# First layer's result turned to channel rows: half of it by VectorE blocks and SBUF-to-SBUF transfers in place of TensorE

## The chip, the core and the metric

The kernel runs on one core of a Trainium2 chip. The metric is the device time of one execution in microseconds (us). Before the change it is 2030.38 us, the median of three runs (2029.91 to 2031.34). The engines are named as the profile names them: PE (TensorE, matmuls; PEld is its weight load), DVE (VectorE), ACT (ScalarE), POOL (GpSimd), SP (the queue that issues almost all transfers).

## What is computed

A decoder of two layers over 256 tokens of 2048 channels, all in float32. The first layer ends with a gated feed-forward network that is added to the residual stream `x`; the second layer begins with three projections of that stream, each behind an RMS norm whose scale is applied later, to the product:

```python
for l in range(DEPTH):
    if l == N_A:                                    # l == 1
        kv = rmsnorm(x, g_kv) @ w_kv_a              # first product of the second layer
        ...
    h = rmsnorm(x, g_mix[l])
    ...
    x = x + conv_ffn(rmsnorm(x, g_ffn[l]), w_ffn_up[l], conv_w[l], conv_b[l], w_ffn_down[l])
return rmsnorm(x, g_final)
```

## The kernel before

**Two layouts.** The products of the second layer want the stream by channels: 128 channels on the partitions, 16 such blocks of 256 tokens. The tile `k.x` (named `xT` in the trace) holds it so. The down-projection of the feed-forward network is computed the other way round: 128 tokens on the partitions, two such halves `tb`, 2048 channels along the row. Its running sum is the tile `xt` (class `Tokens`, line 1345). So between the first layer's feed-forward network and the second layer the stream has to be turned from tokens to channels.

**Split operands.** Every float32 product is made of three passes over rounded pieces. ACT rounds an operand (`hi`), DVE subtracts the rounded part from it (`lo`). Weights are treated so per 128x1024 block: transfer into `raw`, then ACT writes `whi`, then DVE writes `wlo`. `raw` and `whi` have 4 buffers each, so SP can load a block only when DVE is done with the one four blocks earlier. The stream's pieces for the products are in `xhl`, two tiles of eight channel blocks each, `[hi | lo]` per block.

**The end of the first layer's network.** The down-projection runs in two phases, `ph` 0 (channels 0 to 1023) and `ph` 1 (channels 1024 to 2047), for each of three groups of hidden units. In the last group phase 1 goes through six weight chunks, n = 0 to 5, of 24 matmuls of 512 columns each (lines 795 to 797). At its start DVE still adds what phase 0 gave to `xt` (`combine`, recorded under line 1391 with its lambda, and `added`, line 1407). Channels 0 to 1023 are complete with that. Phase 1's own four accumulators, `e00`, `e01`, `e10` and `e11`, are added to `xt` by line 1407 after chunk 5; the figure after `e` is the token half, the last one the column half.

**Turning.** `Inner.turned(k0)` turns two channel blocks: four PE transposes of 128x128 into one PSUM bank (line 406, in `token_transpose`), then ACT rounds the bank into `xhl` (1441), DVE writes the rest (1442), and ACT copies the bank into `k.x` (1443). Four calls, for channel blocks 0 to 7, are hooks behind chunks n = 1 to 4 of phase 1. The other four, for blocks 8 to 15, are hooks behind the first two chunks of the second layer's first product (`k.pending`, 1457). The square sums of the norm come from `xt` itself (1430).

**The first product of the second layer.** `gemm_fm` with `w_kv_a` (line 1140): eight weight chunks of two channel blocks each, 24 matmuls of 256 columns per chunk (lines 157, 158 with `hi` weights, 160 with `lo` weights). Chunk c needs `xhl` of blocks 2c and 2c+1. Its weights go through line 108 (SP), 123 (ACT) and 124 (DVE).

**What sets the order.** A scheduler orders each engine's instructions around here; each engine then works through its own list strictly in order. `keep_in_program_order` pins an instruction among its engine's others.

**A turn by blocks** in the other direction exists already: `Tokens.turn` (1361) turns channels to tokens before the network, with DVE transposes of 32x32 blocks and 4 transfers each from SP that put the blocks in place (1368).

Of the kernel before, what the change touches and what calls it, by code (L numbers as in the profile page):

```python
# [8 lines left out]
F32 = mybir.dt.float32  # L9
# [3 lines left out]
AF = mybir.ActivationFunctionType  # L13
ALU = mybir.AluOpType
AX = mybir.AxisListType

P = 128
D = 2048
S = 256
NB = D // P  # L20
# [1319 lines left out]
class Tokens:  # L1340
# [37 lines left out]
    def begin(self, ph, last):  # L1378
        self.ph, self.last = ph, last
        if ph == 0:  # L1380
            self.staged = self.k.ap.tile([P, 2, 4, 512], F32, tag="xT", name=self.k.uid("staged"))
        return {}
# [38 lines left out]
class Inner(Tokens):  # L1421
    def begin(self, ph, last):
        super().begin(ph, last)
        return {"hooks": {n: [lambda n=n: self.turned(2 * n - 2)] for n in range(1, 5)}} if last and ph else {}

    def evict(self, tb, half, acc):
        j, o = self.added(tb, half, acc)
# [3 lines left out]

    def turned(self, k0):
        k, nc = self.k, self.nc
        if k0 == 0:
            k.new_hl()
            k.x = k.ap.tile([P, NB, S], F32, tag="xT", name=k.uid("xT"))

        def put(b, acc):
            a = acc.rearrange("p (k s) -> p k s", k=2)
            hl = k.hl_tiles[b // 8][:, b % 8 : b % 8 + 2, :]  # L1440
            nc.scalar.activation(hl[:, :, :S], a, AF.Copy)
            nc.vector.tensor_tensor(hl[:, :, S:], a, hl[:, :, :S].bitcast(F32), ALU.subtract)
            nc.scalar.activation(k.x[:, b : b + 2, :], a, AF.Copy)

        k.token_transpose(self.xt, k0, k0 + 2, put)
# [111 lines left out]
```

## Time and profile before

| | |
|---|---|
| median of three runs | 2030.38 us |
| span of the profiled execution, first to last instruction | 2027.8 us |
| what lies around the span, against the median | 2.6 us |
| granted TensorE clock, mean of the span | 0.999 |
| PE / PEld busy | 99% / 94% |
| DVE / ACT / POOL busy | 80% / 58% / 6% |
| DMA: moved, mean rate | 409.24 MB, 202 GB/s |

All queries below have times counted from the start of the span. In a timeline row come the start, the time from the first start to the last end, engine, line, operation, output<-input and how many instructions are merged. Matmuls overlap: one of 512 columns is listed with 0.39 us, but they start 0.23 us apart. In the chain of work that ended last a row has the time by which the chain moved on. The profiled execution's own time outside of the span is not recorded, so sums are made on the span and set against the median with the 2.6 us.

### The profile page before, as it was taken

How to read it: one execution, taken by the hardware profiler on the slowest of the kernel's cores; microseconds unless marked ns; L12 is line 12 of the kernel's file. 1: busy time of each engine (PE TensorE's matmuls, PEld its weight loads, DVE VectorE, ACT ScalarE, POOL GpSimd, SP SyncE). 2: the span in 40 equal slices, each digit the busy share in tenths (PEclk: the TensorE clock that was granted, in tenths of full speed). 3: DMA queues.
4: the chain of work that ended last, by engine and by line, in shares of the span. 5: the costliest groups of instructions: out<-in, count | busy, mean ns of one | idle time of the engine just before them, and what ended most of it. 6: DMA issues, size and time to landing. Idle time of an engine off the chain costs nothing.

```text
span 2027.8 us, 38053 instructions
## 1 busy us (share of the span) xinstructions
PE 2017.2 (99%) x15136; PEld 1912.3 (94%) x15136; DVE 1618.2 (80%) x2433; ACT 1167.1 (58%) x1675; POOL 112.8 (6%) x169
## 2 busy tenths in 40 slices
PE   9999999999999999999999999999999999999998
PEld 8989999999889999899989999999988999889996
DVE  6866766778898788987878786777889878898787
ACT  6754744545565555655566675455566555565565
POOL 0000013100000000000002141400000000000000
PEclk9999999999999999999999999999999999999999
DMA  8876556688657676577656634568865767657764
GB/s 255 234 216 181 166 193 195 192 209 259 208 177 218 198 240 199 179 216 246 187 179 187 183 113 162 190 196 210 257 205 181 219 192 246 196 177 219 241 206 145
DMA packets 248263, 409.24 MB, mean 202 GB/s; under 512 B 71502, under 2 KB 78996, under 8 KB 248084
## 3 DMA queue, kind: packets, MB, share of 16 engines
q1 hardware_dynamic: 247892, 406.27, 65.4%
q8 instruction: 118, 1.93, 0.4%
q14 instruction: 61, 0.50, 0.1%
q10 hardware_dynamic: 192, 0.54, 0.1%
HBM read 400.46 MB, written 2.10 MB: 199 GB/s over the span
## 4 chain that ended last, share of the span: by engine, by line
PE 99%; DVE 0%; ACT 0%; issue 0%; ACTq 0%
PE ps L157 22%; PE ps L158 22%; PE ps L160 22%; PE ps L796 7%; PE ps L797 7%; PE ps L795 7%; PE ps L189 2%; PE ps L190 2%; PE ps L191 2%; PE ps L524 1%; PE ps L406 0%; PE ps L604 0%; PE ps L602 0%; PE ps L603 0%; PE ps L1236 0%; PE ps L1024 0%
## 5 line engine op out<-in xcount | busy, mean ns | idle before, releaser
L118 ACT ACTIVATE whi<-raw 128x1024 fp32r<-128x1024 f32 x484 | 512.7, 1061 | 513.1 <-PE ps L158 373.6
L119 DVE TENSOR_TENSOR wlo<-raw,whi 128x1024 fp32r<-128x1024 f32 x484 | 599.0, 1241 | 246.6 <-ACT whi L118 244.1
L157 PE MATMUL ps<-xhl,whi 128*128 128x256 f32 x3264 | 763.1, 277 | 0.0
L158 PE MATMUL ps<-xhl,whi 128*128 128x256 f32 x3264 | 761.5, 276 | 0.0
L158 PEld LDWEIGHTS ps<-xhl,whi 128*128 128x128 f32 x3264 | 612.8, 188 | 0.5
L157 PEld LDWEIGHTS ps<-xhl,whi 128*128 128x128 f32 x3264 | 612.7, 188 | 0.6
L160 PE MATMUL ps<-xhl,wlo 128*128 128x256 f32 x3264 | 436.6, 276 | 0.0
L160 PEld LDWEIGHTS ps<-xhl,wlo 128*128 128x128 f32 x3264 | 400.5, 188 | 0.0
L710 DVE TENSOR_TENSOR wlo<-raw,whi 128x1024 fp32r<-128x1024 f32 x112 | 134.3, 1220 | 31.5 <-ACT whi L709 30.3
L796 PE MATMUL ps<-wlo,h 128*128 128x512 f32 x404 | 157.3, 390 | 0.0
L797 PE MATMUL ps<-whi,h 128*128 128x512 f32 x404 | 157.2, 389 | 0.0
L709 ACT ACTIVATE whi<-raw 128x1024 fp32r<-128x1024 f32 x112 | 115.7, 1055 | 53.1 <-PE ps L158 37.3
L795 PE MATMUL ps<-whi,h 128*128 128x512 f32 x404 | 128.8, 390 | 0.0
L157 PE MATMUL ps<-mainhl,whi 128*128 128x256 f32 x512 | 119.7, 277 | 0.0
L158 PE MATMUL ps<-mainhl,whi 128*128 128x256 f32 x512 | 119.3, 276 | 0.0
L890 ACT ACTIVATE c<-a,cT 128x256 f32<-128x256 f32 x176 | 99.7, 592 | 32.2 <-DVE a L237 30.2
L709 ACT ACTIVATE whi<-xs 128x1024 fp32r<-128x1024 f32 x52 | 53.8, 1059 | 87.3 <-DVE xs L757 73.1
L158 PEld LDWEIGHTS ps<-mainhl,whi 128*128 128x128 f32 x512 | 96.0, 188 | 0.0
L157 PEld LDWEIGHTS ps<-mainhl,whi 128*128 128x128 f32 x512 | 95.9, 188 | 0.0
L795 PEld LDWEIGHTS ps<-whi,h 128*128 128x128 f32 x404 | 75.8, 188 | 15.7
L797 PEld LDWEIGHTS ps<-whi,h 128*128 128x128 f32 x404 | 75.8, 188 | 15.7
L796 PEld LDWEIGHTS ps<-wlo,h 128*128 128x128 f32 x404 | 75.9, 188 | 15.4
(378 smaller groups left out, 2896.6 us busy)
## 6 DMA issues: line engine op xcount, KB each, us to landing
raw<-in_w_ffn_up SPq DMA_DIRECT2D x352, 512.0 KB, 4.4
raw<-in_w_ffn_down SPq DMA_DIRECT2D x126, 512.0 KB, 4.5
raw<-in_w_out SPq DMA_DIRECT2D x64, 512.0 KB, 3.9
raw<-in_w_in_a SPq DMA_DIRECT2D x56, 512.0 KB, 4.2
gate<-in_w_ffn_down SPq DMA_DIRECT2D x38, 512.0 KB, 4.6
raw<-in_w_mem_kv SPq DMA_DIRECT2D x31, 512.0 KB, 4.8
sums<-in_w_ffn_down SPq DMA_DIRECT2D x48, 256.0 KB, 7.1
raw<-in_w_in_b SPq DMA_DIRECT2D x16, 512.0 KB, 4.1
```

Of the source, the lines that this page charges most:

```text
L118: nc.scalar.activation(hi[:, :n], raw[:, :n], AF.Copy)
L119: nc.vector.tensor_tensor(lo[:, :n], raw[:, :n], hi[:, :n].bitcast(F32), ALU.subtract)
L157: mm(acc[:, :S], wh, x[:, :S], start=first, stop=False)
L158: mm(acc[:, :S], wh, x[:, S:], start=False, stop=False)
L160: mm(acc[:, :S], wl, x[:, :S], start=False, stop=last)
L189: mm(acc, xh, wh, start=first, stop=False)
L709: self.behind(self.nc.scalar.activation(hi, w, AF.Copy))
L710: self.behind(self.nc.vector.tensor_tensor(lo, w, hi.bitcast(F32), ALU.subtract))
L795: mm(o, xh, wh, start=start, stop=False)
L796: mm(o, xh, wl, start=False, stop=False)
L797: mm(o, xl, wh, start=False, stop=stop)
L890: nc.scalar.activation(c, a, AF.Identity, scale=w(2), bias=w(3))
```

## The change

The four calls for channel blocks 0 to 7 go. In their place:

- `blocks(h)`, h = 0 and 1, as hooks behind chunks n = 0 and 1 of phase 1. Each is two DVE transposes (one per token half) of 128x512 in 32x32 blocks from `xt` into a scratch tile `xs`, and 16 transfers of 32 partitions x 8 runs of 32 elements (32 KB, 256 runs of 128 B) from `xs` into `k.x`. h = 0 covers channel blocks 0 to 3 and goes out on POOL's queue; h = 1 covers blocks 4 to 7 and goes out on SP's.
- `operand(b)` for b = 0, 2 as a hook behind chunk 4 and b = 4, 6 behind chunk 5: ACT rounds two blocks of `k.x` into `xhl`, DVE writes the rest. The copy into `k.x` by ACT (1443 before) is no longer needed for these blocks.

Blocks 8 to 15 are turned by PE as before.

```diff
 class Inner(Tokens):
     def begin(self, ph, last):
         super().begin(ph, last)
-        return {"hooks": {n: [lambda n=n: self.turned(2 * n - 2)] for n in range(1, 5)}} if last and ph else {}
+        if not (last and ph):
+            return {}
+        hooks = {h: [lambda h=h: self.blocks(h)] for h in range(2)}
+        hooks.update({n: [lambda b=b: self.operand(b) for b in range(4 * (n - 4), 4 * (n - 3), 2)] for n in (4, 5)})
+        return {"hooks": hooks}
+
+    def blocks(self, h):
+        k, nc = self.k, self.nc
+        if h == 0:
+            k.new_hl()
+            k.x = k.ap.tile([P, NB, S], F32, tag="xT", name=k.uid("xT"))
+        xs = k.tmp(self.pool, [P, 1024], "xs", 2)
+        s = xs.rearrange("p (r k a j) -> p r k a j", r=4, k=4, a=2)
+        for a in range(2):
+            src = self.xt[:, a, 512 * h : 512 * (h + 1)].rearrange("p (k r j) -> p r k j", r=4, j=32)
+            k.tc.keep_in_program_order(nc.vector.transpose(out=s[:, :, :, a], in_=src))
+        for r in range(4):
+            o = k.x[32 * r : 32 * (r + 1), 4 * h : 4 * (h + 1)].rearrange("i k (a q j) -> i q (k a) j", a=2, j=32)
+            for q in range(4):
+                (nc.sync if h else nc.gpsimd).dma_start(out=o[:, q], in_=s[32 * q : 32 * (q + 1), r].rearrange("i k a j -> i (k a) j"))
+
+    def operand(self, b):
+        k, nc = self.k, self.nc
+        x, hl = k.x[:, b : b + 2, :], k.hl_tiles[b // 8][:, b % 8 : b % 8 + 2, :]
+        nc.scalar.activation(hl[:, :, :S], x, AF.Copy)
+        nc.vector.tensor_tensor(hl[:, :, S:], x, hl[:, :, :S].bitcast(F32), ALU.subtract)
```

In `turned` the three lines that made `xhl` and `k.x` at `k0 == 0` go too. Lines behind the insertion move by 22 to 25: the squares (1430 before) are 1455 in the changed kernel, the adds stay 1407.

The scheduler moves work with it, all of it between chunk 0 of phase 1 and the first half of the product with `w_kv_a`; the order elsewhere is the same. PE at the seam of the two layers, before (`ps_12070` is the accumulator `e11`, `ps_12365` and on those of the product, `xhl_12143` the pieces of blocks 0 to 7):

```order
L797 MATMUL ps_12070<-whi_12295,hhx_1502_10099 128x512
L157 MATMUL ps_12365<-xhl_12143,whi_12370 128x256
L158 MATMUL ps_12365<-xhl_12143,whi_12370 128x256
L157 MATMUL ps_12365<-xhl_12143,whi_12370 128x256
L158 MATMUL ps_12365<-xhl_12143,whi_12370 128x256
```

and PE there in the changed kernel (`xhl_12107` the pieces of blocks 0 to 7, `ps_12447` to `ps_12503` the banks of the four turns of blocks 8 to 15):

```order
L797 MATMUL ps_12070<-whi_12305,hhx_1502_10099 128x512
L157 MATMUL ps_12379<-xhl_12107,whi_12384 128x256
L157 MATMUL ps_12380<-xhl_12107,whi_12384 128x256
L157 MATMUL ps_12381<-xhl_12107,whi_12384 128x256
L157 MATMUL ps_12382<-xhl_12107,whi_12384 128x256
L406 MATMUL ps_12447<-ident,xt 128x128 x4
L406 MATMUL ps_12455<-ident,xt 128x128 x4
L406 MATMUL ps_12495<-ident,xt 128x128 x4
L406 MATMUL ps_12503<-ident,xt 128x128 x4
L158 MATMUL ps_12379<-xhl_12107,whi_12384 128x256
```

Four products with `hi` of block 0 now stand ahead of the turns of blocks 8 to 15, which have moved up from behind the second and third chunk of the product; the rest of the first chunk stands behind them.

ACT around the seam in the changed kernel (1448 is the rounding of two blocks from `k.x`, first the pair 0 to 3, then 4 to 7; 123 the weights of the product; 1455 the squares):

```order
L123 ACTIVATE whi_12416<-raw_12415,gT 128x512 x2
L1455 ACTIVATE src_12338,fsums<-xt 128x512
L1448 ACTIVATE xhl_12107<-xT_12110 128x2x256 x2
L1455 ACTIVATE src_12341,fsums<-xt 128x512
L123 ACTIVATE whi_12464<-raw_12463,gT 128x512 x2
L123 ACTIVATE whi_12512<-raw_12511,gT 128x512
L1455 ACTIVATE src_12344,fsums<-xt 128x512
L123 ACTIVATE whi_12512<-raw_12511,gT 128x512
L1455 ACTIVATE src_12347,fsums<-xt 128x512
L1448 ACTIVATE xhl_12107<-xT_12110 128x2x256 x2
```

Before, the four roundings of blocks 0 to 7 (1441) stood one by one among the weights of chunks 3 to 5 of phase 1. Now they stand in two pairs, after the first square and after the last, and DVE's list has the matching subtractions (1449) at the same places, the first pair between the adds of `e10` and `e11`.

SP's list there in the changed kernel (`raw_12383` to `raw_12543` are the first five loads of `w_kv_a`):

```order
L108 DMA raw_12383<-in_w_kv_a 128x2x512
L108 DMA raw_12415<-in_w_kv_a 128x2x512
L108 DMA raw_12463<-in_w_kv_a 128x2x512
L1443 DMA xT_12110<-xs_12166 32x8x32 x16
L108 DMA raw_12511<-in_w_kv_a 128x2x512
L108 DMA raw_12543<-in_w_kv_a 128x2x512
```

Before, the five loads followed one another; now 16 transfers stand between the third and the fourth. On POOL's list the other 16 stand ahead of the fill and the adds with which it prepares the second layer (1098, 1107); nothing else of POOL stands near.

More of the change, by code (lines that the diff above doesn't have):

```diff
@@ L1433, in turned @@
         k, nc = self.k, self.nc
-        if k0 == 0:
-            k.new_hl()
-            k.x = k.ap.tile([P, NB, S], F32, tag="xT", name=k.uid("xT"))
         def put(b, acc):
```

## The prediction

> **What bounds the kernel now.** I read the page first: busy shares, clock and the chain that ended last.
>
> ```profile
> PE 2017.2 (99%) x15136; PEld 1912.3 (94%) x15136; DVE 1618.2 (80%) x2433; ACT 1167.1 (58%) x1675; POOL 112.8 (6%) x169
> PEclk9999999999999999999999999999999999999999
> PE 99%; DVE 0%; ACT 0%; issue 0%; ACTq 0%
> ```
>
> PE is busy for 2017.2 of 2027.8 us at full clock, and the chain runs through PE alone. So an instruction taken off PE is worth its own time on PE, and anything that makes PE wait costs its full length: there is no slack elsewhere to absorb it. Then I read the stretch of the change, first in a table by windows.
>
> ```profile
> 1042.00:1047.00 5.00, 5.00 (x26) 4.11 (x25) 3.63 (x4) 4.89 (x10) 0.00 (x0) 1.00 0.63 204
> 1047.00:1058.00 11.00, 11.00 (x54) 9.11 (x53) 6.29 (x9) 6.73 (x10) 0.00 (x0) 1.00 0.31 96
> 1058.00:1062.00 4.00, 4.00 (x23) 3.42 (x22) 3.36 (x6) 2.99 (x7) 0.00 (x0) 1.00 0.75 216
> ```
>
> The columns are window, length, then PE, PEld, DVE, ACT and POOL busy, clock, DMA share, GB/s. PE has no gap here either. DVE and ACT have some room, POOL does nothing, and the DMA engines are less than a third busy from 1047 to 1058.
>
> **What is removed.** The 16 PE transposes of channel blocks 0 to 7, in the chain of work:
>
> ```profile
> 1037.72 0.11 PE ps L406
> 1041.51 0.33 PE ps L406 x3
> 1043.70 0.44 PE ps L406 x4
> 1049.61 0.44 PE ps L406 x4
> 1055.54 0.43 PE ps L406 x4
> ```
>
> That is 0.11 + 0.33 + 0.44 + 0.44 + 0.43 = **1.75 us** off the chain. The other 16 transposes move up but stay, 8 of them at 0.87:
>
> ```profile
> 1066.90 0.87 PE ps L406 x8
> 1061.28 0.28 PE L157 MATMUL ps<-xhl,whi 128*128 128x256 f32 x1
> 1061.40 0.28 PE L158 MATMUL ps<-xhl,whi 128*128 128x256 f32 x1
> ```
>
> The second of these rows is the first matmul of the product with `w_kv_a`. It can now stand at 1061.28 - 1.75 = **1059.53**. This is the time by which `xhl` of block 0 has to be rounded, and so the time by which POOL's 16 transfers have to be in.
>
> **When POOL can start.** DVE's rows before that:
>
> ```profile
> 1036.59 1.22 DVE L710 TENSOR_TENSOR wlo<-gate,whi 128x1024 fp32r<-128x1024 f32 x1
> 1037.72 0.68 DVE L1407 TENSOR_TENSOR xt<-ps,xt 128x512 f32<-128x512 f32 x1
> 1040.59 1.28 DVE L1407 TENSOR_TENSOR xt<-ps,xt 128x512 f32<-128x512 f32 x2
> L1364 DVE STREAM_TRANSPOSE xs<-xT x8: 1235/1240/1245, 412.5 to 1388.6; 128x1024 f32<-128x1024 f32 x8
> ```
>
> The same transposition takes 1.24 us for 1024 columns, so 0.62 for 512. The first one stands ahead of the row at 1036.59, the second behind the work that ends at 1040.59: 1040.59 + 2 x 0.62 = **1041.8**. Every transfer of the half needs both. The other two transposes follow the weights of chunk 3. Four of them add 2.5 us to DVE, in windows where it was idle for 1.4 and 4.7 us, and each `wlo` then still stands some 2 us ahead of its matmul; I cost them at nothing. The four subtractions have the same size as before, and ACT loses four copies of 0.6 us.
>
> **When POOL's half must be in.** Behind a landing at L stand ACT's two roundings, DVE's two subtractions and, behind these on DVE, the add of `e11`, for which the last two turns on PE wait.
>
> ```profile
> L1441 ACT ACTIVATE xhl<-ps x8: 574/590/600, 1043.5 to 1071.8; 128x512 fp32r<-128x512 f32 x8
> 1067.38 1.09 ACT L1441 ACTIVATE xhl<-ps 128x512 fp32r<-128x512 f32 x2
> 1068.12 1.28 DVE L1442 TENSOR_TENSOR xhl<-ps,xhl 128x512 fp32r<-128x512 f32 x2
> ```
>
> The roundings end at L + 0.6 and L + 1.1, the second subtraction at L + 1.8, the add (0.68) at L + 2.45. PE wants its result behind four matmuls (4 x 0.11) and eight transposes (0.87): 1059.53 + 0.45 + 0.87 = 1060.85. So a landing by **1058.4** costs nothing, and a later one costs what it is late. From 1041.8 that leaves 16.6 us.
>
> **What 16 transfers on POOL's queue take.** No row of before shows a transfer issued by POOL. The nearest rows are SP's:
>
> ```profile
> L1368 SPq DMA_DIRECT2D xt<-xs x32: 591/667/3811, 413.9 to 1398.8; - x32
> 413.87 4.12 SPq L1368 DMA_DIRECT2D xt<-xs  x4
> L399 SPq DMA_DIRECT2D xraw<-in_x x32: 560/625/1169, 26.7 to 61.6; - x32
> DMA to landing us min/median/max: 3.7/3.9/5.3
> 1040.70 7.12 SPq L108 DMA_DIRECT2D raw<-in_w_kv_a  x4
> L1107 POOL TENSOR_TENSOR both<-ident x8: 252/253/257, 1072.0 to 1073.5; 128x32 f32<-128x32 f32 x8
> L279 POOL TENSOR_TENSOR sq<-xT x30: 612/789/1598, 288.7 to 1316.3; 128x256 f32<-128x256 f32 x30
> ```
>
> An issue of SP in the same form (32 partitions, short runs) takes 0.63 to 0.67 us; four in a row take 4.12, which is 1.03 each, since one waited. POOL's own instructions take 0.25 to 1.6 us. So I bound one POOL issue by 0.25 from below and 1.6 from above, and take the mean of the back-to-back row, **1.03**. The landing row belongs to line 399: 3.9 us from issue, reading HBM while the DMA engines were busier. For the last landing here I take 3.0 (an estimate, from that row and the low DMA share of the windows). Then L = 1041.8 + 15 x 1.03 + 3.0 = 1060.25, **1.85 us** late.
>
> The Trainium skill, "DMA: Bandwidth & Descriptors", section "Latency and other measured facts", gives about 0.6 us to the first byte for transfers from SP and ACT and about 1 us for those from GpSimd, whose descriptors software makes. By an estimate with 1 us per issue the half would land 0.45 us earlier, 1.4 late; no run here shows a POOL transfer yet.
>
> **What 16 transfers on SP's queue take.** They wait for DVE's last two transposes, at about 1046.5 by the same addition, and stand ahead of the fourth load of `w_kv_a`. In the row above SP issued the first four loads between 1040.70 and 1047.82; now the fourth comes 16 x 0.42 to 16 x 0.67 = 6.7 to 10.7 us after 1046.5, at the latest at 1057.2. It lands 3.6 to 4 us later, near 1061. PE needs that chunk at 1059.53 + 1.75 + 3 x 2.72 = 1069.4 (24 matmuls at 0.113). ACT has more behind it: two weight halves, two squares, then the roundings of blocks 4 to 7, together 4 us, and PE wants these at 1066.7. Near 1061 leaves about 1.5 us, so I cost SP's half at nothing. At 1.03 per issue the load would land at 1066.6 and PE would wait about 4 us, less what POOL's half has already cost.
>
> **Sum.** 2027.8 - 1.75 + 1.85 = 2027.9 on the span; with the 2.6 us between span and median, **2030.5 us**.
>
> **Rivals.**
>
> *The full gain.* If a POOL issue takes at most (16.6 - 3.0) / 15 = 0.91 us, nothing waits: 2030.4 - 1.75 = **2028.6**. For it speaks that SP's undisturbed issues take 0.67, and that these transfers have a quarter of the runs. Against it, that POOL is not SP, and that its own small jobs reach 1.6.
>
> *POOL's half is far too late.* From (16.6 + 5.75 - 3.0) / 15 = 1.29 us per issue on, PE waits longer than 5.75 us and the kernel is slower by over 4 us. At 1.6 the half lands at 1068.8, 10.4 late: **2039**. The place to see it is PE's first row of line 157 at the seam. For it speaks that nothing covers the wait, since PE's list has nothing but these four matmuls ahead of the turns.
>
> *DVE keeps POOL from its work.* If POOL could make transfers only while DVE is idle, it would have, from 1042 to 1059.5, the 1.37 + 4.71 + about 0.3 us that the windows leave. At 1.03 per issue 16.5 us are needed; the other 10 would come once DVE itself waits for ACT and ACT for POOL, so the half would land near 1072.5, 14 late: **2043**. Against it speaks that POOL's adds ran elsewhere at 0.6 to 1.6 us with DVE 80% busy.
>
> The Trainium skill, "SBUF — State Buffer", section "SBUF: two separate sides", has this as the trap "DVE blocks DMA": some VectorE modes lock GpSimd out while it writes descriptors. The same page says that `tensor_tensor` has no such mode, and DVE's work here is nearly all of that kind, so I give it little.
>
> *SP's weights come late*, as worked out above: at 1.03 per issue about 2 us on top of the forecast, **2032.5**.
>
> **How the numbers follow.** Forecast, POOL late by up to 5.75 us: 0.38. Full gain: 0.33. POOL far too late: 0.20. DVE in the way: 0.05. SP late: 0.04. About 0.2%, 4 us, is what a measurement of this kernel can tell from no change. The whole gain is 1.75 us, so faster than that bound can't come out of any case but a mismeasured one: 0.03. Slower are the two late cases and the tail of the forecast with SP's delay on top, 0.27; within the bound the rest, 0.70. The range has the full gain and the spread of the runs (0.5) at its low end, 2028.0, and the 1.6 us issue at its high end, rounded up to 2040; beyond lies the case of DVE.
>
> **What would show it.** Line 406 with `xt` has 16 matmuls left, and the chain loses 1.75 us between 1037 and 1059. A row of POOL's transfers, from about 1042 on, shows the cadence: up to 0.91 us the first rival is right, near 1.03 the forecast, over 1.29 the second. The wait of PE for ACT's line 1448 at the seam should be some 2 us; with none, the time should be 2028.6. The fourth load of `w_kv_a` should be issued by 1057 and no PE wait should stand behind the first chunk of that product. I am wrong in kind if PE waits for a weight (SP's queue) or for a `wlo` that a DVE transpose has pushed back.

## The result, and the profile after

The changed kernel takes 2036.9 us (median of 6 runs, 2036.07 to 2037.59), the kernel before 2029.95 in the 6 runs beside it: ratio 1.0032, 95% interval 1.0021 to 1.0043. It is **7 us slower**. The profiled execution has a span of 2034.3 us, before 2027.8. The forecast was 2030.5 with a range of 2028.0 to 2040.0: the time is in the range, but beyond the 4 us bound, and not by the mechanism that was given the most weight.

From the page of the changed kernel, the busy row of PE and the chain's shares by engine, then the row of PE's groups where idle time stands behind the last bar:

```profile
PE 2016.6 (99%) x15120; PEld 1911.6 (94%) x15120; DVE 1620.8 (80%) x2437; ACT 1164.8 (57%) x1671; POOL 122.1 (6%) x185
PE 96%; DVE 1%; DMA 1%; ACT 1%; issue 1%; SPq 0%; ACTq 0%; DVEq 0%
L157 PE MATMUL ps<-xhl,whi 128*128 128x256 f32 x3264 | 763.4, 277 | 6.9 <-ACT xhl L1448 6.9
```

The 16 PE instructions are gone (15136 to 15120), but PE is busy for only 0.6 us less, not 1.75, and the chain runs through PE for 96% of its length, before for 99%. There is one new wait, 6.9 us, all of it in one place and all of it for ACT's rounding of the operand. PE's timeline at the seam (start, length, work, and in brackets the idle time ahead of it):

```profile
1059.04 0.39 PE L797 MATMUL ps<-whi,hhx 128*128 128x512 f32 x1
1066.33 1.22 PE L157 MATMUL ps<-xhl,whi 128*128 128x256 f32 x4 [6.91 <-ACT xhl L1448]
1067.36 3.13 PE L406 MATMUL ps<-ident,xt 128*128 128x128 f32 x16
```

The down-projection ends 2.0 us earlier than before, as it should. Then PE stands still. And when it starts again it is slow: the 16 transposes take 3.13 us, where 8 took 0.87 before. The windows say why; the column behind POOL is the granted clock:

```profile
1063.00:1063.50 0.50, 0.00 (x0) 0.00 (x0) 0.50 (x2) 0.50 (x2) 0.00 (x0) 0.53 1.05 406
1063.50:1066.33 2.83, 0.00 (x0) 0.00 (x0) 2.48 (x7) 2.83 (x8) 0.00 (x0) 0.50 0.85 287
1066.33:1069.50 3.17, 3.17 (x15) 3.17 (x16) 1.83 (x5) 1.27 (x3) 0.00 (x0) 0.50 0.71 230
1069.50:1070.00 0.50, 0.50 (x4) 0.50 (x4) 0.34 (x2) 0.50 (x2) 0.00 (x0) 0.64 0.15 57
```

The clock was halved while PE stood idle and stayed so after it had work. From the two edge rows, 0.53 and 0.64, the half clock runs from 1063.03 to 1069.86. PE works in the last 3.53 us of that and loses half of them, 1.76. So the span adds up: 2027.8 - 2.0 + 6.91 + 1.76 = 2034.5, against 2034.3.

What did ACT do while PE waited? Its timeline (left out are the 0.19 us that each square takes to hand over its sum):

```profile
1060.33 1.15 ACT L1448 ACTIVATE xhl<-xT 128x512 fp32r<-128x512 f32 x2 [2.73 <-DMA xT<-xs]
1061.38 0.61 ACT L1455 ACTIVATE src<-xt 128x512 f32<-128x512 f32 x1
...
1061.99 1.93 ACT L123 ACTIVATE whi<-raw,gT 128x512 fp32r<-128x512 f32 x3
1063.83 0.61 ACT L1455 ACTIVATE src<-xt 128x512 f32<-128x512 f32 x1
...
1064.44 0.71 ACT L123 ACTIVATE whi<-raw,gT 128x512 fp32r<-128x512 f32 x1
1065.06 0.61 ACT L1455 ACTIVATE src<-xt 128x512 f32<-128x512 f32 x1
...
1065.67 1.13 ACT L1448 ACTIVATE xhl<-xT 128x512 fp32r<-128x512 f32 x2
```

Line 1448 stands there twice, and it is the second pair, at 1065.67, that releases PE. ACT stands still for 2.73 us, until a transfer lands, and then works through squares and weights without a gap until 1065.67. Which half each pair belongs to, the rows don't say. The semaphores in the program's list of ACT do. Each queue has eight of them, called lanes here: DMAHW for SP's queue, DMASW for POOL's. The list is cut to the two pairs:

```
L1448 ACTIVATE xhl_12107<-xT_12110 128x2x256 [waits DMAHW4_49,DMAHW5_49,DMAHW3_49,DMAHW6_49,DMAHW2_49,DMAHW7_49,DMAHW1_49,DMAHW0_49]
...
L1448 ACTIVATE xhl_12107<-xT_12110 128x2x256 [waits DMASW4_49,DMASW5_49,DMASW3_49,DMASW6_49,DMASW2_49,DMASW7_49,DMASW1_49,DMASW0_49]
```

**The first pair is SP's half**, blocks 4 to 7, and the second is POOL's, blocks 0 to 3, of which PE's first product is made. The trace agrees: that product starts at 1066.33, when the first of the second pair's two roundings (0.61 us) is done. The section on the change has this the wrong way round ("first the pair 0 to 3, then 4 to 7"): the scheduler, not the code's order, had placed them. Last, the transfers (duration min/median/max, first and last start, then times to landing):

```profile
L1443 POOL DMA_DIRECT2D xT<-xs x16: 582/584/750, 1042.4 to 1054.5; - x16
L1443 SPq DMA_DIRECT2D xT<-xs x16: 585/608/881, 1046.3 to 1058.1; - x16
DMA to landing us min/median/max: 1.9/5.5/7.5
1048.45 1.16 POOL L1443 DMA_DIRECT2D xT<-xs  x2 [1.32 <-DMA xT<-xs]
1058.84 7.50 SPq L108 DMA_DIRECT2D raw<-in_w_kv_a  x5
```

POOL issues one in 0.58 us. It waits three times (the row at 1048.45 is the first of them) for an earlier transfer to land, because with eight lanes there are at most eight transfers under way: in POOL's list the ninth transfer waits for the lane of the first, and so on to the sixteenth. Its last one is issued at 1054.5, 3.6 us before the last of SP's, whose half holds up ACT. All 512 packets of POOL's queue (0.53 MB, its 16 transfers) have moved by 1056.5; from there to 1060 only SP's queue moves any. So POOL's half lay ready some 9 us before ACT began to round it. The fourth load of `w_kv_a` goes out at 1058.84, and ACT, which has no gap from 1060.33 on, never waits for it.

**Theory A**: the 6.9 us come from the place that blocks 0 to 3 got in ACT's list: behind SP's half, three sums of squares and the weights of the third and fourth chunk. POOL's half had long landed. **Rival B**: POOL's transfers land late, whatever the list; the packets above already speak against it. **Rival D**: SP's 16 transfers hold back the weights. And apart from these, a **clock theory**: the slow stretch after the wait comes from PE's idleness itself.

### The profile page after: what moved, and what is told of

The parts are those of the page before. It is cut to its first block, busy times and chain, and to the rows that moved or that the text cites. A ratio compares the mean times of both kernels' runs of the same rounds, so it can differ in the third digit from the quotient of the medians.

```text
span 2034.3 us, 38086 instructions
## 1 busy us (share of the span) xinstructions
PE 2016.6 (99%) x15120; PEld 1911.6 (94%) x15120; DVE 1620.8 (80%) x2437; ACT 1164.8 (57%) x1671; POOL 122.1 (6%) x185
## 4 chain that ended last, share of the span: by engine, by line
PE 96%; DVE 1%; DMA 1%; ACT 1%; issue 1%; SPq 0%; ACTq 0%; DVEq 0%
PE ps L157 22%; PE ps L158 22%; PE ps L160 22%; PE ps L795 7%; PE ps L796 7%; PE ps L797 7%; PE ps L189 2%; PE ps L190 2%; PE ps L191 2%; PE ps L524 1%; PE ps L604 0%; DMA xT<-xs 0%; PE ps L602 0%; PE ps L603 0%; PE ps L1236 0%
## 5 line engine op out<-in xcount | busy, mean ns | idle before, releaser
L797 PE MATMUL ps<-whi,h 128*128 128x512 f32 x404 | 157.2, 389 | 0.0
L124 DVE SCALAR_TENSOR_TENSOR wlo<-raw,gT,whi 128x512 fp32r<-128x512 f32 x96 | 71.7, 784 | 24.0 <-ACT whi L123 23.9
L797 PEld LDWEIGHTS ps<-whi,h 128*128 128x128 f32 x404 | 75.9, 188 | 15.7
```

The costliest lines, as they stand in the source:

```text
L124: nc.vector.scalar_tensor_tensor(lo[:, s], raw[:, s], gains[k], hi[:, s].bitcast(F32), ALU.mult, ALU.subtract)
L797: mm(o, xl, wh, start=False, stop=stop)
```

## The experiments

All times are medians beside runs of the kernel before on the same chip. For every run the span can be set against a sum of three terms: what the seam gains, what PE waits, and half of the time in which PE works at half clock. These sums hold for the one profiled execution, whose own time can lie below the median (by 1.3 us in e2, by 2.0 in e4). What an execution loses or gains elsewhere is not in them.

### e1: POOL's half first in ACT's list

```diff
     def operand(self, b):
-        nc.scalar.activation(hl[:, :, :S], x, AF.Copy)
+        with k.tc.issue_after(self.first) if b else nullcontext():
+            a = nc.scalar.activation(hl[:, :, :S], x, AF.Copy)
+        if b <= 2:
+            self.first = a.ins
...
+            with self.behind():
                 self.nc.scalar.activation(junk, o, AF.Square, accum_out=self.sums[:, tb, j : j + 1])
...
+        rest = self.behind()
+        k.pending[2].append(rest.__enter__)
+        k.pending[3] = [lambda: rest.__exit__(None, None, None)]
```

`issue_after` puts what is traced inside it behind one instruction on that instruction's engine; `behind()` is the same with `self.first`. The last lines put ACT's work for the fourth chunk of `w_kv_a` behind it too.

> The changed kernel with one thing altered: ACT rounds blocks 0 to 3 (POOL's half) ahead of blocks 4 to 7 (SP's half), and both ahead of the four sums of squares and of the fourth weight chunk of w_kv_a. Theory A (the 6.9 us wait of PE comes from ACT's list: blocks 0 to 3 stood behind SP's half and behind the late fourth load, while POOL's half had long landed): the roundings start near 1056.5, PE's wait at the seam falls to at most 1.2 us, the clock stays at 1.00, 2028.0 to 2029.7 us. Rival B (POOL's half itself lands late, the order does not matter): PE still waits 5 us or more, 2034 or more. Rival C (ACT as such has no room here): a wait of 2 to 4 us moves to another row, about 2032.

Measured: 2029.16 us, ratio 0.9997 (0.9988 to 1.0005), span 2027.2. That is 7.7 us less than the changed kernel, with the same transfers on the same queues. ACT and PE:

```profile
1058.73 1.33 ACT L123 ACTIVATE whi<-raw,gT 128x512 fp32r<-128x512 f32 x2 [2.88 <-PE ps L797]
1059.97 2.18 ACT L1449 ACTIVATE xhl<-xT 128x512 fp32r<-128x512 f32 x4
1060.64 0.74 PE L157 MATMUL ps<-xhl,whi 128*128 128x256 f32 x4 [1.27 <-ACT xhl L1449]
1061.22 1.91 PE L406 MATMUL ps<-ident,xt 128*128 128x128 f32 x16
```

The wait is 1.27 us and the 16 transposes are back at 1.91: no half clock. (1.2 us at most was expected, and the roundings from 1056.5.) Sum: 2027.8 - 2.0 + 1.27 = 2027.1, span 2027.2. Rival B has fallen, and so has Rival C: PE has no other wait between 1030 and 1100. What is left of the wait is again the list: the roundings stand behind the weights of the third chunk, for whose tile ACT waits 2.88 us until PE has read what was in it (L797).

### e2: the two queues exchanged

```diff
-                (nc.sync if h else nc.gpsimd).dma_start(out=o[:, q], in_=s[32 * q : 32 * (q + 1), r].rearrange("i k a j -> i (k a) j"))
+                (nc.gpsimd if h else nc.sync).dma_start(out=o[:, q], in_=s[32 * q : 32 * (q + 1), r].rearrange("i k a j -> i (k a) j"))
```

> The changed kernel with the two queues exchanged: SP issues blocks 0 to 3, POOL blocks 4 to 7. ACT's list then has blocks 0 to 3 ahead of the first weight chunk, and blocks 4 to 7 behind the last transposes. SP's 16 transfers would be issued from 1042.3 to about 1054.5 and land near 1056.7. Theory A: the half that PE needs first is the one that ACT rounds first, so PE waits at most 1 us at the seam, 2028 to 2031. Rival B (a POOL transfer is slow by itself): blocks 4 to 7 arrive late and PE waits 3 us or more behind the second chunk, 2033 or more. Rival D (SP's 16 transfers in front of three weight loads are what costs): PE waits for a whi or wlo of w_kv_a, 2032 or more.

Measured: 2032.96 us, ratio 1.0013 (1.0004 to 1.0022), span 2029.9. A miss for all three as written. No wait at the seam, as Theory A said, but two waits 7 us later, for POOL's half:

```profile
1066.23 1.53 ACT L1463 ACTIVATE xhl<-ps 128x512 fp32r<-128x512 f32 x3
1067.66 1.14 ACT L1448 ACTIVATE xhl<-xT 128x512 fp32r<-128x512 f32 x2
1068.34 0.74 PE L157 MATMUL ps<-xhl,whi 128*128 128x256 f32 x4 [2.05 <-ACT xhl L1448]
1069.86 0.58 PE L158 MATMUL ps<-xhl,whi 128*128 128x256 f32 x1 [0.78 <-DVE xhl L1449]
L1443 POOL DMA_DIRECT2D xT<-xs x16: 582/582/745, 1046.7 to 1055.5; - x16
```

POOL's transfers aren't late. POOL issued its last at 1055.5, and ACT does not wait ahead of the row of 1448: it is busy with the turned blocks 8 to 13, which stand ahead of blocks 4 to 7 in its list, though PE wants blocks 4 to 7 first. In both kernels the list has SP's half ahead of POOL's. Here ACT was behind besides: it had stood still for 5.21 us until SP's half was in at 1054.5, and for 0.58 us for the second load of `w_kv_a`, and no run separates that from the order. A gap of 2.05 us and the first half microsecond of the next were enough to halve the clock for one window:

```profile
1066.21:1069.62 3.41, 0.82 (x5) 0.53 (x4) 3.41 (x6) 3.41 (x8) 2.59 (x9) 1.00 0.90 304
1069.50:1070.00 0.50, 0.14 (x1) 0.14 (x1) 0.50 (x2) 0.50 (x2) 0.00 (x0) 0.62 0.91 320
...
1073.00:1073.50 0.50, 0.50 (x5) 0.50 (x5) 0.00 (x0) 0.50 (x2) 0.00 (x0) 0.97 0.00 0
```

Half clock from 1069.62 to 1073.03, 3.41 us; PE had work for 3.17 of it. Sum: 2027.8 - 2.0 + 2.83 + 1.58 = 2030.2, span 2029.9.

### e3: no transfers

```diff
-        s = xs.rearrange("p (r k a j) -> p r k a j", r=4, k=4, a=2)
+        s = k.x[:, 4 * h : 4 * (h + 1)].rearrange("p k (r a j) -> p r k a j", r=4, a=2)
...
-                (nc.sync if h else nc.gpsimd).dma_start(out=o[:, q], in_=s[32 * q : 32 * (q + 1), r].rearrange("i k a j -> i (k a) j"))
```

> Leaves out the 32 transfers: DVE's transposes write straight into the operand tile, so the 32x32 blocks are not put in their places and the values are not the reference's. DVE's four transposes, ACT's four roundings and DVE's four subtractions remain. Every theory in which the transfers (their landing, their queues, or the place that ACT gave to what waits for them) cost the time: no wait at the seam, the whole gain of 1.75 to 2.0 us, 2028.0 to 2028.4. If DVE's transposes themselves delay PE: 2030 or more.

Measured: 2028.38 us (2027.39 to 2030.45), ratio 0.9994 (0.9985 to 1.0003), span 2025.8, no wait of PE between 1030 and 1100. So 2.0 us is what there is to gain at the seam (2027.8 - 2.0 = 2025.8), and DVE's four transposes cost PE nothing.

### e4: POOL's half alone

```diff
-        hooks = {h: [lambda h=h: self.blocks(h)] for h in range(2)}
-        hooks.update({n: [lambda b=b: self.operand(b) for b in range(4 * (n - 4), 4 * (n - 3), 2)] for n in (4, 5)})
+        hooks = {0: [lambda: self.blocks(0)], 3: [lambda: self.turned(4)],
+                 4: [lambda: self.operand(0), lambda: self.operand(2), lambda: self.turned(6)]}
```

> Only blocks 0 to 3 go by DVE and POOL's queue; blocks 4 to 7 are transposed by PE as in the kernel before, so SP's queue has only its loads and the fourth one is issued near 1047.5 again. ACT's list has the two roundings behind the fourth weight chunk and behind three sums of squares. Theory A: no wait for SP's half and no late load, but the place in ACT's list stays bad: the roundings start at 1061.5 to 1062.5, PE waits 1.5 to 2.5 us at the seam, below the length at which the clock fell, 2030.5 to 2032. Rival B (POOL late by itself): 5 us or more of wait, 2034 or more. If the order in ACT's list does not matter: 2029.1, half the gain.

Measured: 2035.61 us (2032.53 to 2040.72), ratio 1.0028 (1.0018 to 1.0038), span 2031.6. ACT and PE:

```profile
1061.67 1.32 ACT L123 ACTIVATE whi<-raw,gT 128x512 fp32r<-128x512 f32 x2
1062.90 1.14 ACT L1447 ACTIVATE xhl<-xT 128x512 fp32r<-128x512 f32 x2
1063.57 0.74 PE L157 MATMUL ps<-xhl,whi 128*128 128x256 f32 x4 [3.20 <-ACT xhl L1447]
L1442 POOL DMA_DIRECT2D xT<-xs x16: 582/584/745, 1042.3 to 1053.5; - x16
```

With neither SP's half nor a late load, PE still waits 3.2 us, while ACT does the weights of the third and fourth chunk and the squares that its list has ahead. I expected 1.5 to 2.5, and full clock. The clock fell all the same, at 1064.65, when PE had been at work again for 1.1 us, and stayed down for 3.41 us (from the edge windows, 0.65 in the half microsecond from 1064.50 and 0.94 in that from 1068.00). The down-projection's last matmul starts at 1059.98, before at 1061.06, so 1.1 us is gained here. Sum: 2027.8 - 1.1 + 3.20 + 1.71 = 2031.6, span 2031.6. The median is 2.0 us above this execution; it reaches the 2034 that Rival B named, but the wait is 3.2 us and not 5, and POOL's last packets moved by 1055.5. So the list costs 3.2 us by itself. What the 6.91 us have beyond that fits SP's half: ACT's 2.73 us until it landed and its two roundings (1.15 us) are not in e4's list.

### e5: nothing ahead of POOL's half

```diff
-        k.pending[2].append(rest.__enter__)
+        k.pending[1].append(rest.__enter__)
```

This is e1 with the weights of the third chunk behind the roundings too.

> As e1, and ACT's roundings also stand ahead of the weights of the third chunk of w_kv_a: in e1 they waited behind those (1058.73, for a weight tile that PE freed with its last matmul before the seam), which left 1.27 us of wait. Theory A: no wait at the seam (at most 0.2 us), clock 1.00, the whole gain, 2027.8 to 2028.4 us, as e3 gave without any transfer. Rival (POOL's half lands only at 1059 to 1060, and the row in e1 named the wrong cause): the wait stays at 1.0 to 1.3, 2029.2.

Measured: 2027.53 us (2027.05 to 2030.01), ratio 0.9990 (0.9981 to 0.9999), span 2025.5.

```profile
1056.21 1.16 ACT L1449 ACTIVATE xhl<-xT 128x512 fp32r<-128x512 f32 x2 [0.29 <-DMA xT<-xs]
1059.28 0.63 PE L157 MATMUL ps<-xhl,whi 128*128 128x256 f32 x4
1059.39 1.15 ACT L1449 ACTIVATE xhl<-xT 128x512 fp32r<-128x512 f32 x2 [2.02 <-DMA xT<-xs]
1059.00:1062.00 3.00, 3.00 (x27) 2.92 (x27) 2.52 (x5) 2.61 (x6) 0.00 (x0) 1.00 0.93 279
```

The row at 1056.21 is the measurement that the prediction wanted: **POOL's half is in at 1056.2**, 2.2 us ahead of the limit of 1058.4. SP's half is in at 1059.4, and PE's first product starts at 1059.28 without a wait. The transfers and their queues are those of the changed kernel; the list alone made the difference between the two.

### e6: PE kept busy in its wait

```diff
...
         accs = [self.psum() for _ in range(nblk)]
+        for _ in range(fill):
+            self.tc.keep_in_program_order(self.nc.tensor.transpose(accs[0][:, :P], self.ident, self.ident))
```

with `fill=60` for this one product.

> The changed kernel with 60 transposes of the identity on PE (about 6.5 us) between the last matmul of the down-projection and the first of w_kv_a, in what was PE's wait; their results are overwritten. ACT's list is as in the changed kernel, so the first product still starts near 1066.3. Clock theory (PE's half speed after the seam is a clock that was lowered because PE stood idle): clock 1.00 throughout, transposes of xt 0.11 apart, 2035.0 to 2035.5 us, some 1.7 below the changed kernel. Rival (PE is slow after the seam because of what it waits for, operands or memory traffic): the clock and the spacing as in the changed kernel, 2036.5 to 2037.5.

Measured: 2034.16 us, ratio 1.0024 (1.0014 to 1.0033), span 2032.2.

```profile
1059.35 6.71 PE L166 MATMUL ps<-ident 128*128 128x128 f32 x60
1065.82 0.72 PE L157 MATMUL ps<-xhl,whi 128*128 128x256 f32 x4
1066.00:1071.00 5.00, 5.00 (x46) 5.00 (x45) 2.55 (x4) 2.42 (x4) 0.00 (x0) 1.00 0.35 107
```

The clock stays at 1.00 and the product runs at its usual pace. PE starts it at 1065.82, 0.5 earlier than in the changed kernel; this time the 60 transposes set the start, since ACT began the pair of roundings for blocks 0 to 3 at 1064.37, 1.3 earlier. The span is 2.1 shorter: 0.5, and 1.6 that the half clock would have cost (1.76 in the changed kernel). In the sum the 6.47 us of the transposes take the place of the wait: 2027.8 - 2.0 + 6.47 = 2032.3, span 2032.2. The slow stretch is the clock's, and the clock follows PE's idleness. The median came out under the expected 2035.0, by this half microsecond and the scatter of the runs.

### e7 and e8: SP's half alone, and all 32 transfers on SP's queue

```diff
-        hooks = {h: [lambda h=h: self.blocks(h)] for h in range(2)}
-        hooks.update({n: [lambda b=b: self.operand(b) for b in range(4 * (n - 4), 4 * (n - 3), 2)] for n in (4, 5)})
+        hooks = {1: [lambda: self.turned(0), lambda: self.blocks(1)], 2: [lambda: self.turned(2)],
+                 5: [lambda: self.operand(4), lambda: self.operand(6)]}
...
```

> Only blocks 4 to 7 go by DVE and SP's queue; blocks 0 to 3 are transposed by PE as in the kernel before. ACT's list has the two roundings behind the second weight chunk and ahead of the last sums of squares and the third chunk. Theory A (SP's half costs only through what ACT queues behind it and ahead of blocks 0 to 3): PE's first product needs nothing of it, so no wait over 0.5 us and half the gain, 2028.9 to 2029.5. Rival D (SP's 16 transfers make the fourth weight load late enough for PE): PE waits for a whi or wlo of w_kv_a, 2031 or more.

```diff
-                (nc.sync if h else nc.gpsimd).dma_start(out=o[:, q], in_=s[32 * q : 32 * (q + 1), r].rearrange("i k a j -> i (k a) j"))
+                nc.sync.dma_start(out=o[:, q], in_=s[32 * q : 32 * (q + 1), r].rearrange("i k a j -> i (k a) j"))
```

> All 32 transfers on SP's queue, none on POOL's. By the cadence of SP in the changed kernel and in e2 (16 in 10.6 to 12.4 us) they run from 1041.4 to about 1063, and the second, third and fourth load of w_kv_a stand behind them. Theory D (what the queue holds back decides): PE waits some 4 to 6 us for the weights of the second chunk, loaded from about 1063 and rounded near 1067.5, the clock falls for 3.4 us, 2033 to 2036. Rival (SP's issue is not the limit, loads arrive in time): 2030 or less.

Measured: e7 2028.61 us, ratio 0.9994 (0.9985 to 1.0002), span 2026.9, no wait of PE: half the gain (2027.8 - 0.9), at the edge of the expected 2028.9 to 2029.5. In its list the roundings stand where nobody suffers from them. e8 2034.28 us, ratio 1.0023 (1.0013 to 1.0033), span 2032.2. SP's queue and PE's waits in e8:

```profile
1063.77 2.08 SPq L108 DMA_DIRECT2D raw<-in_w_kv_a  x4
1067.26 0.70 PE L270 MATMUL ps<-ssum,ones 128*128 128x256 f32 x2 [2.95 <-ACT xT L1465]
1069.15 0.58 PE L157 MATMUL ps<-xhl,whi 128*128 128x256 f32 x1 [1.18 <-ACT whi L123]
```

With 32 transfers ahead the second load of `w_kv_a` goes out at 1063.77, as expected, and PE waits 1.18 us for its weights, rounded from 1068.4 on. The 2.95 before that are ACT's list again: a copy out of PSUM stood behind the roundings that waited for the last of the 32. So Rival D is a real mechanism, but it took all 32, and only 1.18 of the 4.13 us of waiting are its own, though the time is the one that it named. With 16, in e5, the fourth load goes out at 1057.90, about 1 us earlier than in the changed kernel, and PE waits for nothing.

### e9 and e10: e5 and the changed kernel once more

> e5 unaltered, beside the changed kernel on the same chip, to see whether its gain holds. If the whole gain is 2.0 us at the seam, as PE's first product at 1059.28 (before 1061.28) says: 2027.5 to 2028.3, ratio 0.9985 to 0.9995. If e5's 2027.53 was chance: within 0.5 us of the kernel before.

> The changed kernel unaltered. The terms at the seam (2.0 off, 6.9 of wait, 1.7 of half clock) add up to 6.6 us: ratio 1.0028 to 1.0036, and 8 to 9 us above e9. If the clock's share is not fixed, since the clock is lowered and raised in steps of 3.4 us that need not fall at the same place of the kernel each time, the single times spread over 1.5 us or more.

Measured: e9 2028.55 us (2027.25 to 2033.63), ratio 0.9994 (0.9985 to 1.0002); e10 2037.4 us (2035.67 to 2040.26), ratio 1.0036 (1.0024 to 1.0048). e5's version gained 2.4 us once and 1.5 once, with intervals that touch or all but touch 1: it beats the changed kernel by 9 us, and the kernel before by about its 2.0 us, which one such comparison can hardly tell from none. e9's median is 0.25 us above what was expected. Its profiled execution has no wait of PE at the seam either, but a span of 2027.1, 1.6 more than e5's: 0.8 of that is there 10 us after the start, 0.8 comes in the second layer, far from the seam, and these runs don't show why. The profiled execution of e10 has a span of 2036.2, 1.9 above that of the changed kernel, at an unchanged start of PE's first product (1066.33):

```profile
1066.33 1.23 PE L157 MATMUL ps<-xhl,whi 128*128 128x256 f32 x4 [6.42 <-ACT xhl L1448]
1062.00:1062.50 0.50, 0.00 (x0) 0.00 (x0) 0.50 (x2) 0.50 (x2) 0.00 (x0) 0.57 1.08 414
1066.00:1072.00 6.00, 5.67 (x26) 5.67 (x27) 3.88 (x9) 4.10 (x9) 0.92 (x4) 0.50 0.47 151
1072.00:1072.50 0.50, 0.50 (x5) 0.50 (x4) 0.50 (x1) 0.36 (x1) 0.50 (x4) 0.69 0.00 0
```

This time the half clock ran from 1062.07 to 1072.31, 10.24 us, three times 3.41. PE worked in the last 5.98 of them and lost 2.99, not 1.76. So a wait that ends at the same time costs 1.2 us more or less, by where the clock's windows fall. The other 0.7 of the 1.9 came at full clock, in the product behind; its cause is open. Single times of e10 spread over 4.6 us, as the second case of its expectation said, but those of e9 spread over 6.4, so the spread is no proof of the clock; the two profiled executions are.

## Why the prediction was right in its range and wrong in its mechanism

**What is removed: right.** 1.75 us was forecast, 2.0 came (e3; PE's first product at 1059.28 in e5, forecast 1059.53, before 1061.28).

**When POOL can start: right.** 1041.8 forecast, 1042.35 measured. DVE's transposes of 512 columns take 0.70 us, not 0.62, and delayed no matmul.

**What 16 transfers take: mis-sized, and to the other side.** 1.03 us per issue and 3.0 for the landing gave 1060.25. An issue takes 0.58, but the eight lanes hold POOL up three times, so the 16 spread over 12.1 us in the changed kernel. The half was in at 1056.2 in e5, and by 1056.5 in the changed kernel. By my own limit of 1058.4, nothing should have waited: with that term right, the sum would have said 2028.6, further from the result. So would the sign that the forecast named: first to last issue, 12.1 us over 15, is 0.81 each, which is the full gain's side. The other price, 1 us per issue, took a time to the first byte for the time of an issue.

**The step that failed** is the one behind it: "Behind a landing at L stand ACT's two roundings". It takes for granted that ACT does them when the transfers land. In ACT's list nine instructions stood ahead of them, the first of which waited for SP's half, and 6.91 us of PE's time hung on that. The two rows of line 1448 in the list read alike, and I took the first for blocks 0 to 3 because the code traces them first. The limit of 1058.4 has the same fault: the subtractions that stand ahead of the add of `e11` in DVE's list are those of SP's half. The order of a list that a scheduler makes has to be read from what each row waits for.

**SP's half "at nothing": wrong, for a reason that I had not looked at.** The forecast asked whether PE wants blocks 4 to 7 and the fourth chunk in time; it did have them in time. But ACT waited for SP's half with blocks 0 to 3 queued behind. The fourth load went out at 1058.84, forecast 1057.2 at the latest: 16 issues at 0.67 (10.7 us) were assumed as the worst, and 12.4 us came, since SP too waits for its lanes, 1.7 us here.

**A wait costs "what it is late": wrong.** 6.91 us of wait cost 8.7, and 6.42 in e10 cost 9.4. Every rival with a wait was priced too low by this. The Trainium skill, "TensorE: Matmul & The Clock Gate", section "Part 1: The HAM clock gate", has the rule: PE's activity is watched over free-running windows of 3413 ns, the clock is halved after an idle one, and a busy one restores it. The trace agrees to the digit on the window (3.41, 6.83 and 10.24 us of half clock), and e6 agrees on the cause. On how idle and how busy a window must be, the runs say more than the rule, as the last section shows. It is the rule against this change that the prediction should have weighed.

**The rivals.** The full gain is what the transfers' own timing bears out, and e5 shows it. "POOL's half is far too late" has the size (over 4 us, and PE's wait above 5.75) but not the cause. DVE did not keep POOL from issuing: 582 to 750 ns each beside a busy DVE. SP's late weights took 32 transfers to become real. The case that happened, a rounding that is ready and stands in the wrong place of its engine's list, was not among them. That the range held is luck: its high end was set by another mechanism, which happened to have a similar size.

## What to carry to other kernels

When work leaves the engine that bounds the kernel, its result often reaches that engine through another one's in-order list: read there, row by row and with the semaphores, what stands ahead of the new instruction, before working out when its data arrive. Where a scheduler makes the list, give it the order (here, pinning ACT's roundings turned 7 us of loss into about 2 of gain). And price a wait of PE of two microseconds or more with one to three windows of half clock on top; here they cost 1.6 to 3.0 us.

## What the runs showed of the hardware that was not expected

The granted clock is halved and restored in steps of 3.41 us, at a phase that differs between executions. In the 3.41 us ahead of the drop PE was busy for 0.82 us in e2 (a gap of 2.05 and the start of the next), for 1.08 in e4, where PE was at work again when the clock fell, and for 1.25 in e10. In e1 a gap of 1.27 us, which leaves at least 2.14 of 3.41, left the clock alone. So a full idle window isn't needed; where between 1.25 and 2.14 us the limit lies, these runs don't tell. Nor does any work restore the clock: in e10 PE was busy for 2.56 of the second 3.41 us of half clock, and the clock stayed down for a third, while 3.17 of 3.41 restored it in e2.

The time that a transfer takes to land varied from run to run on either queue: the medians are 2.2 to 5.5 us on POOL's and 1.9 to 3.8 on SP's, with the high ends in the changed kernel. From the DMA view of e4, e2 and e7, median us from issue to landing of the same 32 KB:

```profile
xT<-xs POOLq DMA_DIRECT2D x16, 32.0 KB, 5.0
xT<-xs POOLq DMA_DIRECT2D x16, 32.0 KB, 2.2
xT<-xs SPq DMA_DIRECT2D x16, 32.0 KB, 1.9
```

In e4 SP issues loads of 512 KB from 1041.0 on, beside POOL's transfers; in e2 it issues none between 1041.1 and 1052.7. With eight lanes to a queue, 5 us a landing is also what slows the issue: in e4 POOL waited for landings and took 11.8 us for its 16, in e2 it issued them in 9.4 us without a wait. That the loads are the cause is inferred from these two runs; no run changed the loads alone.
